# The low rope-key product of two neighbouring heads as 64-row products on the two halves of the array

## The chip, the cores and the metric

The kernel runs on one core of one Trainium2 chip. The time is the device time of one execution in microseconds (us); the time before is the median of three runs. A core has a matrix engine (PE, which loads weights, called PEld in the profile, and then streams columns through them), VectorE (DVE), ScalarE (ACT), GpSimd (POOL) and SyncE (SP), which only issues transfers here. Each engine works through its own list in order, and waits where an instruction needs another engine's result.

## The reference

One layer of a mixer with two groups of heads; 1024 latent tokens, 128 context tokens, 256 cached keys. The part that the change touches is the attention of the latent tokens, four heads of 128 plain and 64 rotary dimensions:

```python
def one_block(i):                       # 128 queries
    for qr, (kn, kr, _) in zip(q_ropes, key_sets):
        ...
        logits.append(jnp.einsum('bqhn,bkhn->bhqk', qn, kn)
                      + jnp.einsum('bqhr,bkr->bhqk', qrb, kr))
    s = jnp.concatenate(logits, axis=-1).astype(jnp.float32) * ATTN_SCALE
    p = jax.nn.softmax(s, axis=-1).astype(v_all.dtype)
    return jnp.einsum('bhqk,bkhv->bqhv', p, v_all)
```

The rotary key `kr` is one for all four heads. The first key set are the 1024 latent keys (rotated), the second the 256 cached ones (not rotated). Around this stand a projection, a gated position mixing and an output projection, which do not change.

## The kernel before

**Numbers in two parts.** Products run on values rounded to a short form (F32R). To keep precision each operand is split into a high and a low part, and a product is made of high x high, high x low and low x high.

**The score operands.** For each block `t` of 128 queries and each head `h`, `qnh` and `qnl` hold the high and low part of the query, already carried into the latent space of the keys (128 rows). `qr` holds both parts of the 64 rotary dimensions on top of one another in 128 rows: an even head has the high part in rows 0 to 63 and the low one in rows 64 to 127, an odd head the other way round. `kch` and `kcl` are the parts of the latent key; `krh` and `krl` hold the parts of the rotary key, each of them twice, in rows 0 to 63 and again in 64 to 127. So the product of `qr` with `krh` gives high x high and low x high at once, and the one with `krl` gives high x low and, beside it, low x low. `logits` makes these five products into one bank of PSUM, the accumulator memory.

**The steps.** `score_steps(t, h)` gives the steps of one head: `lat(0)` and `lat(1)` for the two halves of 512 latent keys, into a tile `s1` of two banks (two such tiles are in turn, so a head's tile is needed again two heads later), and `con` for the 256 cached keys, into its half of the one tile `s2`. `softmax` sets up what follows on the other engines, to be recorded some time later by a planning clock (`later(dt, fn)`): DVE takes the maximum of the latent scores (`start`, L1440), then that of the cached ones and the bias `nb` (`shift`, L1443 to L1448), ACT two exponentials into `e` (L1458: 256 columns, then 1024), DVE the reciprocal of the sum, POOL the division (L1463).

**The values.** `value_steps` handles a pair of heads: five times four transposes of `e` (L1524, tile `pT`), which ACT copies to `ph` (L1528) and DVE subtracts to `pl` (L112), six value products into `o` (L1548 to L1550), and at the end a product with `wuv` (L1567, tile `at`).

**The order.** The order on each engine is the one in which the steps are recorded; no scheduler moves it. There are 32 heads, eight query blocks of four. The scores run ahead: `merged` lays the scores of one pair of heads between the value steps of an earlier pair, in proportion to the planned cost of each step. In the same stage ACT, DVE and POOL also prepare the output projection's weights (tiles `traw`, `thi`, `wor`), which SP loads.

Of the kernel before, what the change touches and what calls it, by code (L numbers as in the profile page):

```python
# [9 lines left out]
F32 = mybir.dt.float32  # L10
# [8 lines left out]
P = 128  # L19
# [6 lines left out]
CTX0 = 9 * P  # L26
# [68 lines left out]
def tile_hymba_step(ctx: ExitStack, tc: tile.TileContext, I, O):  # L95
    nc = tc.nc
    V, S, G, T = nc.vector, nc.scalar, nc.gpsimd, nc.tensor

    def opened(name, bufs=1, space=None, side=None):
        kw = dict(name=name, bufs=bufs, reuse_waits="tile")  # L100
        if space is not None:
            kw["space"] = space
        if side is not None:
            kw["side"] = side
        cm = tc.tile_pool(**kw)
        return cm, cm.__enter__()

    def closed(cm):
        cm.__exit__(None, None, None)
# [57 lines left out]
    def later(dt, fn):  # L167
        waiting.append((now[0] + dt, fn))
        waiting.sort(key=lambda w: w[0])
# [42 lines left out]
    def merged(a, b):  # L212
        ta, tb = sum(x for x, _ in a) or 1.0, sum(x for x, _ in b) or 1.0
        ia = ib = 0
        da = db = 0.0
        while ia < len(a) or ib < len(b):
            if ib >= len(b) or (ia < len(a) and da / ta <= db / tb):
                da += a[ia][0]
                run(a[ia])
                ia += 1  # L220
            else:
                db += b[ib][0]
                run(b[ib])
                ib += 1
# [403 lines left out]
    with tc.manual_schedule(engines=engines):  # L628
        keep_warm(WARM0)
        start = Plan()  # L630
# [598 lines left out]
    qnh, qnl, qr = {}, {}, {}  # L1229
# [12 lines left out]
    rot = {}  # L1242
# [114 lines left out]
    if True:  # L1357
# [25 lines left out]
        kch = kv.tile([P, 11 * P], F32R, tag="kch", name="kch")  # L1383
        kcl = kv.tile([P, 11 * P], F32R, tag="kcl", name="kcl")
        krh = kv.tile([P, 11 * P], F32R, tag="krh", name="krh")
        krl = kv.tile([P, 11 * P], F32R, tag="krl", name="krl")
# [36 lines left out]
    c_ps, pss = opened("pss", bufs=2, space=PSUM)  # L1423
# [4 lines left out]
    s2 = pss.tile([P, 2, 256], F32, tag="s2", name="s2", bufs=1)  # L1428

    def softmax(t, h, lat_, con_):  # L1430

        m = sm.tile([P, 2], F32, tag="m", name=f"m{t}{h}", bufs=3)
        nb = sm.tile([P, 1], F32, tag="nb", name=f"nb{t}{h}", bufs=3)
        su = sm.tile([P, 2], F32, tag="su", name=f"su{t}{h}", bufs=3)
        rs = sm.tile([P, 1], F32, tag="rs", name=f"rs{t}{h}", bufs=3)
        e = ap_.tile([P, 1280], F32, tag="e", name=f"e{t}{h}", bufs=6)
        es[t, h] = e

        def start():
            V.tensor_reduce(m[:, 0:1], lat_, axis=AX.X, op=ALU.max)  # L1440

        def shift():
            V.tensor_reduce(m[:, 1:2], con_, axis=AX.X, op=ALU.max)  # L1443
            if units or t < 2 or (t, h) == (NS - 1, 3):
                V.tensor_reduce(nb, m, axis=AX.X, op=ALU.max)
                V.tensor_scalar(nb, nb, nscl[:, t : t + 1], None, op0=ALU.mult)  # L1446
            else:
                V.scalar_tensor_tensor(nb, m[:, 0:1], m[:, 1:2], nscl[:, t : t + 1], op0=ALU.max, op1=ALU.mult)  # L1448
            apart = t > 0
            last = (t, h) == (NS - 1, 3)  # L1450
            later(0.5 if last else 1.2 if apart else 0.6, lambda: exp(0))
            later(2.3 if apart else 0.6, lambda: exp(1))
            later(3.9 if apart else 3.1 if t == 0 else 2.5, divide)
            later(1.3, lambda: spare_lo(1))

        def exp(i):
            src, sl = ((con_, slice(1024, 1280)), (lat_, slice(0, 1024)))[i]
            S.activation(e[:, sl], src, AF.Exp, bias=nb, scale=scl[:, t : t + 1], accum_out=su[:, i : i + 1])  # L1458

        def divide():  # L1460
            V.tensor_tensor(rs, su[:, 0:1], su[:, 1:2], op=ALU.add)
            V.reciprocal(rs, rs)
            G.tensor_scalar(e, e, rs, 0.0, op0=ALU.mult, op1=ALU.add)  # L1463
            made.add(("e", t, h))
            spare_hi(1 if his and his[0] in heavy else 2)
            spare_lo(2)
            if units and units[0][0] in traw:
                n_ = 1
                paced[0] += 1
                for i in range(n_):  # L1470
                    unit_of[0](*units.pop(0), 2.2 * i)

        return start, shift

    def logits(ps, qs, sl):
        qh_, ql_, qr_ = qs
        T.matmul(ps, qh_, kch[:, sl], start=True, stop=False)  # L1477
        T.matmul(ps, qh_, kcl[:, sl], start=False, stop=False)  # L1478
        T.matmul(ps, ql_, kch[:, sl], start=False, stop=False)  # L1479
        T.matmul(ps, qr_, krh[:, sl], start=False, stop=False)  # L1480
        T.matmul(ps, qr_, krl[:, sl], start=False, stop=True)  # L1481

    def score_steps(t, h):
        g, j = t // 3, t % 3
        sl = slice(j * P, (j + 1) * P)
        a, b = qnh[g][:, h, sl], qnl[g][:, h, sl]
        unrot = qr[g][:, 1, h, sl]
        c_ = s2[:, h % 2, :]
        rot = qr[g][:, 0, h, sl]
        cell = {}  # L1490

        def lat(half):
            if half == 0:
                cell["s"] = pss.tile([P, 2, 512], F32, tag="s1", name=f"s1{t}{h}", bufs=2)
            logits(cell["s"][:, half, :], (a, b, rot), slice(half * 512, half * 512 + 512))
            if half == 1:
                cell["start"], cell["shift"] = softmax(t, h, cell["s"].rearrange("p a c -> p (a c)"), c_)
                later(1.2, cell["start"])

        def con():  # L1500
            logits(c_, (a, b, unrot), slice(CTX0, CTX0 + 256))
            later(0.95 if t else 0.7, cell["shift"])

        return [(1.08, lambda: lat(0)), (1.08, lambda: lat(1)), (0.55, con)]

    otile = {}

# [67 lines left out]
    whole = [area[g].rearrange("p a c -> p (a c)") for g in range(3)]  # L1575
# [19 lines left out]
    def spare_hi(n):  # L1595
        for _ in range(min(n, len(his))):
            his.pop(0)()

    def spare_lo(n):
        for _ in range(min(n, len(los))):  # L1600
            los.pop(0)()
# [46 lines left out]
    LEAD = 2  # L1648
# [70 lines left out]
    heads = [(t, h) for t in range(NS) for h in range(4)]  # L1719
# [19 lines left out]
    def value_stream(pair, drain=False):  # L1739
        it = value_steps(*pair)  # L1740
        steps = []
        for i in range(it[0]):
            steps.append((0.44, lambda i=i: it[1](i)))
            items.append((it, i, i == it[0] - 1))
            advance(steps)
        if drain:
            advance(steps, drain=True)
        return steps

    with tc.manual_schedule(engines=engines):  # L1750
# [79 lines left out]
        def t_load(u):  # L1830
            k, c = divmod(u, 2)
            raw = traw[u] = tp.tile([P, 4, 256], F32, tag="raw", name=f"traw{u}", bufs=2)
            for i, row in enumerate((k, k + 4)):
                nc.sync.dma_start(raw[:, 2 * i : 2 * i + 2, :], I["w_o"][row].rearrange("p (s c) -> p s c", s=2)[:, :, 256 * c : 256 * c + 256])
# [81 lines left out]
                T.matmul(ps, b, woh[k][:, c0:c1], start=False, stop=k == NK - 1)  # L1916

        own = own_steps()
        first = [s_ for i in range(LEAD) for s_ in score_steps(*heads[i])]
        merged(first[:4] + own[:1] + [(0.45, lambda: q_rope_T(7))] + first[4:], [])  # L1920
        for c in range(len(pairs)):
            sc = [s_ for i in (2 * c + LEAD, 2 * c + LEAD + 1) if i < len(heads) for s_ in score_steps(*heads[i])]
            if c == 0:
                sc = sc[:3] + own[1:2] + sc[3:5] + own[2:3] + sc[5:]
            if not sc:
                break
            if c == 1:
                vs = value_stream(pairs[0])
                merged(sc[:2] + own[3:] + vs[:1] + sc[2:3] + vs[1:2] + sc[3:5], [])
                merged(vs[2:], sc[5:])  # L1930
            else:
                merged(sc, value_stream(pairs[c - 1]) if c > 0 else [])
            if 2 * c + LEAD + 1 == 5:
                closed(c_ra)
                c_tp, tp = opened("tp", side="left")
                for u in range(2):
                    t_load(u)
                units += [(u, part) for u in range(8) for part in range(2)]
                unit_of.append(t_unit)
            if 2 * c + LEAD + 1 == 27:  # L1940
                first_jobs()
            if 2 * c + LEAD + 1 == 23:
                for k in range(3):
                    wo_piece(2 + k, *flat[1][2 * k : 2 * k + 2])
# [167 lines left out]
    for q in range(3, len(queue)):  # L2112
        n, name, _ = queue[q]
        cell = {}
        ready = {"S1": "s0", "S2": "s1", "S3": "s2", "S4": "s3"}.get(name)
        deps = [f"{ready}{n}"] if ready and n else []
        room = [name_of(q - 3)]
# [274 lines left out]
```

## Time and profile before

| | |
|---|---|
| median of three runs | 604.39 us (603.84 to 604.91) |
| profiled execution | 604.54 us |
| its span, first to last instruction | 602.8 us |
| granted clock of PE | 0.998 |
| heads 6 to 29 in it | 335.89 to 480.59 us |

The span is what the profile covers; the execution's own time has a little around it. The page lists busy times by engine and groups of instructions by line, operation and tile, written output<-input. The timeline shows single instructions, start and duration in microseconds. The list of waits names who waited for whom, with the total, the count and the longest. Durations of products are modelled to their ends and overlap, so that the distance between two starts tells what one costs in a row. "Issue" is idle time for which no wait shows.

### The profile page before, as it was taken

Reading aid. Unit: us, or ns where it says so; the run is one execution under the profiler, and the core shown is the slowest. Engines: PE = TensorE matmul, PEld = TensorE weight load, DVE = VectorE, ACT = ScalarE, POOL = GpSimd, SP = SyncE. Lnnn points to the kernel's source line nnn. Section 1 sums busy time; section 2 is a strip of 40 time slices with the busy share of each in tenths; the row PEclk is TensorE's granted clock in tenths of the full one; section 3 lists DMA queues with packets and bytes.
Section 4 is the critical chain, followed back from the end, with each engine's and each line's share of the span. In section 5 each row is a group of like instructions: output and inputs, shape, how many; then the busy total and the mean of one; then the engine's idle time right before and its main releaser. Section 6 shows DMA issues by size and latency. Waiting matters only on the chain.

```text
span 602.8 us, 10190 instructions
## 1 busy us (share of the span) xinstructions
PE 592.7 (98%) x3661; PEld 535.6 (89%) x3661; DVE 427.1 (71%) x940; ACT 333.5 (55%) x773; POOL 213.5 (35%) x251
## 2 busy tenths in 40 slices
PE   8999999999999999999999999999999999999995
PEld 8578889999989999999998999999999998888884
DVE  3666888967646368476678677777788876477885
ACT  6565886434323245455567657665656463457543
POOL 2462103200000000343264254545434447259834
PEclk9999999999999999999999999999999999999999
DMA  8992001032052134100002033434232028951444
GB/s 309 375 348 93 1 2 70 1 139 71 18 201 79 55 93 139 41 1 1 1 8 71 1 120 109 149 116 152 76 125 102 1 71 293 368 177 38 143 147 162
DMA packets 31059, 67.33 MB, mean 112 GB/s; under 512 B 3344, under 2 KB 17440, under 8 KB 29984
## 3 DMA queue, kind: packets, MB, share of 16 engines
q1 hardware_dynamic: 27792, 55.93, 26.6%
q0 software_dynamic: 2352, 8.39, 4.1%
q10 hardware_dynamic: 864, 2.36, 1.2%
q8 instruction: 29, 0.48, 0.3%
q14 instruction: 22, 0.18, 0.1%
HBM read 53.45 MB, written 13.21 MB: 111 GB/s over the span
## 4 chain that ended last, share of the span: by engine, by line
PE 91%; DMA 3%; DVE 2%; POOL 2%; ACT 1%; issue 1%; SPq 0%; POOLq 0%; ACTq 0%
PE p L916 14%; PE tp L937 7%; PE pT L1524 5%; PE s L1477 3%; PE s L1478 3%; PE s L1480 3%; PE s L1479 3%; PE s L1481 3%; PE o L1548 3%; PE o L1549 3%; PE o L1550 3%; PE zacc L1349 2%; PE zacc L1348 2%; PE zacc L1350 2%; PE S L1886 2%; PE S L1885 2%
## 5 line engine op out<-in xcount | busy, mean ns | idle before, releaser
L1463 POOL TENSOR_SCALAR e<-e,rs 128x1280 f32<-128x1280 f32 x32 | 47.2, 1474 | 99.0 <-ACT ph L1528 51.7
L112 DVE TENSOR_TENSOR pl<-pT,ph 128x512 fp32r<-128x512 f32 x81 | 55.5, 687 | 31.3 <-ACT ph L1528 31.3
L1528 ACT CAST ph<-pT 128x512 fp32r<-128x512 f32 x80 | 47.2, 590 | 50.6 <-PE pT L1524 50.0
L1458 ACT ACTIVATE e<-s,nb,scl 128x256 f32<-128x256 f32 x64 | 56.9, 890 | 26.0 <-DVE nb L1446 17.3
L1196 POOL TENSOR_TENSOR kr<-z,rope 128x64 f32<-128x64 f32 x8 | 2.6, 326 | 155.3 <-ACT z L1205 155.3
L937 PE MATMUL tp<-area,w 128*128 128x384 f32 x288 | 52.5, 337 | 0.0
L937 PEld LDWEIGHTS tp<-area,w 128*128 128x128 f32 x288 | 50.4, 188 | 0.0
L1548 PE MATMUL o<-ph,vh 128*128 128x256 f32 x160 | 48.4, 302 | 0.0
L1524 PE MATMUL pT<-ident,e 128*128 128x128 f32 x320 | 47.9, 272 | 0.0
L1549 PE MATMUL o<-pl,vh 128*128 128x256 f32 x160 | 45.0, 281 | 0.0
L1550 PE MATMUL o<-ph,vl 128*128 128x256 f32 x160 | 44.9, 281 | 0.0
L1440 DVE TENSOR_REDUCE m<-s 128x1 f32<-128x1024 f32 x32 | 38.9, 1215 | 2.6 <-PE s L1481 2.6
L1524 PEld LDWEIGHTS pT<-ident,e 128*128 128x128 f32 x320 | 37.7, 140 | 2.6
L1477 PE MATMUL s<-kch,area 128*128 128x512 f32 (+2 forms) x100 | 39.2, 392 | 0.0
L1478 PE MATMUL s<-kcl,area 128*128 128x512 f32 (+2 forms) x100 | 35.4, 354 | 0.0
L1480 PE MATMUL s<-krh,area 128*128 128x512 f32 (+2 forms) x100 | 35.3, 353 | 0.0
L1479 PE MATMUL s<-kch,area 128*128 128x512 f32 (+2 forms) x100 | 35.1, 351 | 0.0
L1481 PE MATMUL s<-krl,area 128*128 128x512 f32 (+2 forms) x100 | 35.0, 350 | 0.0
L1548 PEld LDWEIGHTS o<-ph,vh 128*128 128x128 f32 x160 | 30.1, 188 | 1.8 <-ACT os L1558 0.2
L1549 PEld LDWEIGHTS o<-pl,vh 128*128 128x128 f32 x160 | 30.2, 189 | 1.3
L1550 PEld LDWEIGHTS o<-ph,vl 128*128 128x128 f32 x160 | 30.1, 188 | 0.0
L916 PE MATMUL p<-area,w 128*128 128x384 f32 x144 | 27.7, 338 | 0.0
(687 smaller groups left out, 1741.4 us busy)
## 6 DMA issues: line engine op xcount, KB each, us to landing
ada<-in_ada_ss SPq DMA_DIRECT2D x16, 512.0 KB, 6.8
w2r<-in_w_t SPq DMA_DIRECT2D x12, 512.0 KB, 4.9
x<-in_x SPq DMA_DIRECT2D x9, 512.0 KB, 8.3
adag<-in_ada_g SPq DMA_DIRECT2D x4, 1024.0 KB, 4.8
traw<-in_w_o SPq DMA_DIRECT2D x16, 256.0 KB, 3.5
tdram<-thi SPq DMA_DIRECT2D x32, 128.0 KB, 1.8
tdram<-traw SPq DMA_DIRECT2D x32, 128.0 KB, 1.9
wor<-in_w_o SPq DMA_DIRECT2D x8, 512.0 KB, 3.7
```

Of the source, the lines that this page charges most:

```text
L112: V.tensor_tensor(lo, src, f32(hi), op=ALU.subtract)
L916: T.matmul(banks[key], a_, b_, start=k == 0 and m == 0, stop=k == 3 and m == len(passes) - 1)
L937: T.matmul(tps[c, 2][:, :GW], w_[c][:, k, :], x_[k, 2], start=k == 0 and m == 0, stop=k == NK - 1 and m == 2)
L1458: S.activation(e[:, sl], src, AF.Exp, bias=nb, scale=scl[:, t : t + 1], accum_out=su[:, i : i + 1])
L1477: T.matmul(ps, qh_, kch[:, sl], start=True, stop=False)
L1478: T.matmul(ps, qh_, kcl[:, sl], start=False, stop=False)
L1479: T.matmul(ps, ql_, kch[:, sl], start=False, stop=False)
L1480: T.matmul(ps, qr_, krh[:, sl], start=False, stop=False)
L1524: T.transpose(ps[:, w : w + P], es[t, h][:, c * P : (c + 1) * P], ident)
L1548: T.matmul(o, vh[:, kt, :], ph[:, sl], start=c == 0, stop=False)
L1549: T.matmul(o, vh[:, kt, :], pl[:, sl], start=False, stop=False)
L1550: T.matmul(o, vl[:, kt, :], ph[:, sl], start=False, stop=c == n - 1)
```

## The change

For heads 6 to 29 (`FROM`, `UPTO`), twelve of the sixteen pairs, a pair is scored as a whole. `whole` makes four of the five latent products of a head and half; the fifth, with `krl`, becomes `half`: 64 rows of `qr`, those that hold the head's high part (rows 0 to 63 for the even head, 64 to 127 for the odd one), with the same rows of `krl`. The four of them stand in one block, `halves`, between the even head's cached scores and the odd head's latent ones, even and odd in turn. They close the even head's banks and open the odd head's. The low x low part, which the 128-row product had carried along, is left out for the latent keys. The cached keys still go through `logits`. Outside the twelve pairs `plain_steps`, the old code, is used.

```diff
-    def score_steps(t, h):
+    AFTER = 1.7
+    FROM, UPTO = 6, 30
+    def score_steps(t, h0):
+        hs = (h0, h0 + 1)
...
+        def whole(x, ps, c, rot):
+            h = hs[x]
+            a, b, r = qnh[g][:, h, sl], qnl[g][:, h, sl], qr[g][:, 1 - rot, h, sl]
+            T.matmul(ps, a, kch[:, c], start=x == 0, stop=False)
+            T.matmul(ps, a, kcl[:, c], start=False, stop=False)
+            T.matmul(ps, b, kch[:, c], start=False, stop=False)
+            T.matmul(ps, r, krh[:, c], start=False, stop=x == 1)
+        def half(x, ps, c, rot):
+            rows = slice(64 * x, 64 * x + 64)
+            T.matmul(ps, qr[g][rows, 1 - rot, hs[x], sl], krl[rows, c], start=x == 1, stop=x == 0)
+        def halves():
+            e_, o_ = room(0), room(1)
+            for i in range(2):
+                half(0, e_[:, i, :], LATS[i], 1)
+                half(1, o_[:, i, :], LATS[i], 1)
+            after(0)
+            later(0.75, cell["start0"])
+            later(AFTER, cell["shift0"])
...
+        return [
+            *((0.93, lambda i=i: lat(0, i)) for i in range(2)), (0.55, lambda: con(0)), (0.7, halves),
+            *((0.93, lambda i=i: lat(1, i)) for i in range(2)), (0.55, lambda: con(1)),
+        ]
+    def plain_steps(t, h):
...
+    def pair_scores(i):
+        return score_steps(*heads[i]) if FROM <= i < UPTO else [s_ for h in range(2) for s_ in plain_steps(*heads[i + h])]
```

The odd head's maximum and bias are recorded 1.05 and 0.95 behind its last steps (1.2 and 0.95 before). What follows shows the order at the pair of block 2, heads 0 and 1; `s120` and `s121` are their score tiles, `pT10`, `ph10` and `pl10` belong to the pair that is turned into values beside them, `o1` is its output.

PE, the even head's second half, before:

```order
L1477 MATMUL s120_3838<-kch_3222,area0_118 128x512
L1478 MATMUL s120_3838<-kcl_3223,area0_118 128x512
L1479 MATMUL s120_3838<-kch_3222,area0_118 128x512
L1480 MATMUL s120_3838<-krh_3224,area0_118 128x512
L1481 MATMUL s120_3838<-krl_3225,area0_118 128x512
L1548 MATMUL o0_3642<-ph01_4_3823,vh_3226 128x256
```

and in the changed kernel:

```order
L1503 MATMUL s120_3838<-kch_3222,area0_118 128x512
L1504 MATMUL s120_3838<-kcl_3223,area0_118 128x512
L1505 MATMUL s120_3838<-kch_3222,area0_118 128x512
L1506 MATMUL s120_3838<-krh_3224,area0_118 128x512
L1586 MATMUL pT10_1_3871<-ident_75,e10_3572 128x128
```

The product with `krl` is gone from the run of five, and a group of transposes that stood ahead of it now stands behind.

PE, behind the even head's cached scores (`s2`), before:

```order
L1480 MATMUL s2_3381<-krh_3224,area0_118 128x256
L1481 MATMUL s2_3381<-krl_3225,area0_118 128x256
L1548 MATMUL o1_3927<-ph10_0_3852,vh_3226 128x256
L1549 MATMUL o1_3927<-pl10_0_3853,vh_3226 128x256
L1550 MATMUL o1_3927<-ph10_0_3852,vl_3227 128x256
```

and in the changed kernel, four transposes later:

```order
L1586 MATMUL pT10_2_3904<-ident_75,e10_3572 128x128
L1586 MATMUL pT10_2_3904<-ident_75,e11_3625 128x128
L1510 MATMUL s120_3838<-krl_3225,area0_118 128x512
L1510 MATMUL s121_3912<-krl_3225,area0_118 128x512
L1510 MATMUL s120_3838<-krl_3225,area0_118 128x512
L1510 MATMUL s121_3912<-krl_3225,area0_118 128x512
L1610 MATMUL o1_3929<-ph10_0_3851,vh_3226 128x256
```

The four 64-row products stand between the transposes and the value products, and they write the two heads' tiles in turn.

DVE, the even head's maximum (`m20`) and bias (`nb20`), before:

```order
L1440 TENSOR_REDUCE m20_3879<-s120_3838 128x1
L1461 TENSOR_TENSOR rs13_3801<-su13_3800 128x1
L1462 RECIPROCAL rs13_3801<-rs13_3801 128x1
L112 TENSOR_TENSOR traw0_3689<-traw0_3689,thi01_3889 128x512
L112 TENSOR_TENSOR pl10_2_3913<-pT10_2_3907,ph10_2_3912 128x512
L1443 TENSOR_REDUCE m20_3879<-s2_3381 128x1
L1445 TENSOR_REDUCE nb20_3880<-m20_3879 128x1
```

and in the changed kernel:

```order
L1461 TENSOR_TENSOR rs13_3808<-su13_3807 128x1
L1462 RECIPROCAL rs13_3808<-rs13_3808 128x1
L112 TENSOR_TENSOR traw0_3689<-traw0_3689,thi01_3894 128x512
L112 TENSOR_TENSOR pl10_2_3910<-pT10_2_3904,ph10_2_3909 128x512
L1440 TENSOR_REDUCE m20_3917<-s120_3838 128x1
L1443 TENSOR_REDUCE m20_3917<-s2_3381 128x1
L1445 TENSOR_REDUCE nb20_3918<-m20_3917 128x1
```

The maximum of the latent scores went from ahead of the two subtractions to behind them.

More of the change, by code (lines that the diff above doesn't have):

```diff
@@ L1481, in logits, with room, after, lat @@
         T.matmul(ps, qr_, krl[:, sl], start=False, stop=True)
-    def score_steps(t, h):
+    AFTER = 1.7
+    FROM, UPTO = 6, 30
+    LATS = (slice(0, 512), slice(512, 1024))
+    CONS = slice(CTX0, CTX0 + 256)
+    def score_steps(t, h0):
+        g, j = t // 3, t % 3
+        sl = slice(j * P, (j + 1) * P)
+        hs = (h0, h0 + 1)
+        cell = {}
+        def room(x):
+            if x not in cell:
+                cell[x] = pss.tile([P, 2, 512], F32, tag="s1", name=f"s1{t}{hs[x]}", bufs=2)
+            return cell[x]
+        def whole(x, ps, c, rot):
[16 more added lines that the diff above has]
+            later(AFTER, cell["shift0"])
+        def after(x):
+            cell[f"start{x}"], cell[f"shift{x}"] = softmax(t, hs[x], room(x).rearrange("p a c -> p (a c)"), s2[:, x, :])
+        def lat(x, i):
+            whole(x, room(x)[:, i, :], LATS[i], 1)
+            if x and i:
+                after(1)
+                later(1.05, cell["start1"])
+        def con(x):
+            h = hs[x]
+            logits(s2[:, x, :], (qnh[g][:, h, sl], qnl[g][:, h, sl], qr[g][:, 1, h, sl]), CONS)
+            if x:
+                later(0.95 if t else 0.7, cell["shift1"])
+        return [
[3 more added lines that the diff above has]
+    def plain_steps(t, h):
         g, j = t // 3, t % 3
@@ L1918, in tile_hymba_step @@
         own = own_steps()
-        first = [s_ for i in range(LEAD) for s_ in score_steps(*heads[i])]
+        first = pair_scores(0)
         merged(first[:4] + own[:1] + [(0.45, lambda: q_rope_T(7))] + first[4:], [])
         for c in range(len(pairs)):
-            sc = [s_ for i in (2 * c + LEAD, 2 * c + LEAD + 1) if i < len(heads) for s_ in score_steps(*heads[i])]
+            sc = pair_scores(2 * c + LEAD) if 2 * c + LEAD < len(heads) else []
             if c == 0:
```

## The prediction

> **What bounds the kernel now.** I read the page's head first, then PE's waits, then the stretch of the twelve pairs that change, then single instructions in it.
>
> ```profile
> span 602.8 us, 10190 instructions
> PE 592.7 (98%) x3661; PEld 535.6 (89%) x3661; DVE 427.1 (71%) x940; ACT 333.5 (55%) x773; POOL 213.5 (35%) x251
> ```
>
> The matrix engine (PE) is busy for 98% of the span. These are all of its waits in the list of waits:
>
> ```profile
> PE warm L442 <- DVE onesr L239: 1.4, 1, 1.4
> PE modp L337 <- DMA ada<-in_ada_ss: 0.9, 2, 0.5
> PE vacc L436 <- DVE area L112: 0.3, 1, 0.3
> ```
>
> None lies among the scores. The busy times by stretch, from the first product of head 6 to the first of head 30, agree: PE 144.70 of 144.70 us at a granted clock of 1.00, while VectorE (DVE) has 33 us to spare.
>
> ```profile
> core 0: us, PE busy (x) PEld busy (x) DVE busy (x) ACT busy (x) POOL busy (x), PEclk, DMA share, GB/s
> 335.89:480.59 144.70, 144.70 (x1011) 133.40 (x1010) 111.50 (x234) 89.46 (x183) 65.77 (x69) 1.00 0.30 99
> ```
>
> So a pair of heads takes 144.70 / 12 = 12.06 us, and what changes here is worth what it takes from PE or adds to it, as long as no other engine comes late. A busy PE is not the same as an array without gaps, so I price a product by the distance of starts, not by its duration. Five score products of 512 columns in a row, PE's timeline:
>
> ```profile
> 342.25 0.40 PE L1477 MATMUL s<-kch,area 128*128 128x512 f32 x1
> ...
> 343.18 0.39 PE L1481 MATMUL s<-krl,area 128*128 128x512 f32 x1
> 343.41 0.60 PE L1567 MATMUL at<-os,wuv 128*128 128x128 f32 x4
> ```
>
> From 342.25 to 343.41 are five products: 0.232 us each, though each is shown as 0.39 long; the other 0.16 overlaps the next one.
>
> **The change, part by part.** *Removed:* the low product with krl on all 128 rows, once per head and half, so 4 per pair and 48 in all, which is what the groups of that stretch count:
>
> ```profile
> L1481 PE MATMUL s<-krl,area 128*128 128x512 f32 x48 | 18.7, 390 | 0.0
> ```
>
> 4 x 0.232 = 0.93 us of PE time per pair. *Added:* four products of 64 rows and 512 columns in one block. If the two that lie on different halves of the array run side by side, they make two rounds; if not, four. No 64-row product is in this trace, so I take the nearest rows: the gate products gps (L1014) of another stage, whose weights are only 32 columns wide, so that four fit on the array beside one another. PE's timeline in narrow windows, and the weight loads (PEld) at both borders:
>
> ```profile
> 161.61 1.21 PE L916 MATMUL p<-area,w 128*128 128x384 f32 x6
> 162.49 0.33 PE L916 MATMUL p<-area,w 128*128 128x384 f32 x1
> 162.75 0.42 PE L1014 MATMUL gps<-adag,csp 128*32 128x256 f32 x4
> 162.99 0.61 PE L1014 MATMUL gps<-adag,csp 128*32 128x256 f32 x8
> 163.20 0.61 PE L1014 MATMUL gps<-adag,csp 128*32 128x256 f32 x8
> 163.42 0.40 PE L1014 MATMUL gps<-adag,csp 128*32 128x256 f32 x4
> 163.75 0.44 PE L916 MATMUL p<-area,w 128*128 128x384 f32 x1
> 164.03 0.33 PE L916 MATMUL p<-area,w 128*128 128x384 f32 x1
> 162.75 0.16 PEld L1014 LDWEIGHTS gps<-adag,csp 128*32 128x32 f32 x8 [0.25 <-issue]
> 163.75 0.19 PEld L916 LDWEIGHTS p<-area,w 128*128 128x128 f32 x1 [0.41 <-issue]
> ```
>
> Three things are in these rows. First, strips do run together: four products start within the same 0.02 us, and the rounds follow at 162.99, 163.20 and 163.42, 0.215 us apart, where one of them alone lasts 0.40. Second, going into strips and out again costs time. Plain products come every (1.21 - 0.33) / 5 = 0.176 us. From the last plain start before (162.49) to the second after (164.03) are 1.54 us; two plain steps (0.352) and four rounds (0.86) explain 1.21, so the excursion costs 0.33. Third, the weight loads wait at both borders for the array to run empty (the two "issue" gaps) and are then in the open: the first products last 0.42 instead of 0.40 behind a load of 32 columns, and 0.44 instead of 0.33 behind one of 128. The new block loads 128 columns on both sides, so I add 0.11 - 0.02 = 0.09: 0.42 us per block.
>
> A round is 0.215 by the strips and 0.232 by the score products; nothing decides, so I take the middle, 0.224. One block then costs 2 x 0.224 + 0.42 = 0.87 us against the 0.93 removed. The gain is 0.06 us per pair, 0.7 us over twelve. Bounds: at best 0.93 - 0.43 - 0.33 = 0.17 per pair, 2.0 us in all (load price of the narrow strips); at worst the two halves' weights are loaded one after the other, another 0.11 (0.53 in all), with rounds of 0.232, which loses 0.06 per pair, 0.8 us.
>
> The Trainium skill, "TensorEngine Tiling (Array Packing)", Key Properties, states that changing the tiling mode, as against the tile, drains the engine. The strips' 0.33 us agrees for strips of columns; by that rule halves of rows pay too (my forecast), without it the block is the first rival below.
>
> *Another neighbour.* The block stands between transposes and value products. Passing from transposes to products is free in itself:
>
> ```profile
> 350.20 0.60 PE L1524 MATMUL pT<-ident,e 128*128 128x128 f32 x4
> 350.55 0.48 PE L1477 MATMUL s<-kch,area 128*128 128x512 f32 x1
> 350.87 0.40 PE L1478 MATMUL s<-kcl,area 128*128 128x512 f32 x1
> ```
>
> One transpose of 128 columns follows another after (0.60 - 0.27) / 3 = 0.11 us (0.27 is one alone, its group's mean is 272 ns). Four of them and one product of 0.232 make 0.67, which is 350.87 - 350.20.
>
> *Moved:* the maximum of the even head (L1440). Its scores were complete before its context product; now they are complete behind the block, and DVE takes the maximum behind the third pl instead of ahead of two subtractions. On ACT one thi copy goes ahead of the odd head's large exponential and ph number 1 behind it; POOL and SP keep their orders, so the loads and the POOL work start where they did in the program. Queued behind the later maximum are the bias nb, both exponentials, and behind those the next pair's first product, which needs the score bank. One even head before, PE, DVE and ACT:
>
> ```profile
> 375.69 0.39 PE L1481 MATMUL s<-krl,area 128*128 128x512 f32 x1
> 376.31 1.21 DVE L1440 TENSOR_REDUCE m<-s 128x1 f32<-128x1024 f32 x1
> 377.44 0.15 DVE L1461 TENSOR_TENSOR rs<-su 128x1 f32<-128x1 f32 x1
> ...
> 378.31 0.68 DVE L112 TENSOR_TENSOR pl<-pT,ph 128x512 fp32r<-128x512 f32 x1
> 378.91 0.41 DVE L1443 TENSOR_REDUCE m<-s 128x1 f32<-128x256 f32 x1
> 379.55 0.21 DVE L1446 TENSOR_SCALAR nb<-nb,nscl 128x1 f32<-128x1 f32 x1
> 379.80 0.57 ACT L1458 ACTIVATE e<-s,nb,scl 128x256 f32<-128x256 f32 x1 [1.72 <-DVE nb L1446]
> 381.23 1.21 ACT L1458 ACTIVATE e<-s,nb,scl 128x1024 f32<-128x1024 f32 x1
> 384.11 0.40 PE L1477 MATMUL s<-kch,area 128*128 128x512 f32 x1
> ```
>
> The large exponential ends at 382.44 and PE wants the bank at 384.11: 1.67 us of cover. The pl at 378.31 is tied to its transposes and hardly moves, so the maximum (377.44 - 376.31 = 1.13) now goes between it and 378.91, and nb and both exponentials come 1.13 later. The pair is 0.06 shorter. Cover left: 1.67 - 1.13 - 0.06, about 0.5 us. So I cost the move at nothing; it is thin, and below it each 0.1 us short costs 12 x 0.1.
>
> Sum: 0.7 us less. The profiled execution took 604.54 with a span of 602.8, so 1.7 lie around it, and it stands 0.15 above the median 604.39. From the median: **603.7 us**.
>
> **The rivals.**
> - *No price for the mode.* If halves of rows need no emptying, as the transposes above need none, the block costs only its rounds: 0.93 - 0.45 = 0.48 per pair, 5.8 us, 598.6. For it: both kinds use all 128 columns, and the strips do not. Against it: the strips are the only rows in which the array is divided, and they pay on both sides.
> - *The halves run one after the other* (slower). The strips that ran together wrote different partitions; the two halves write the same 128 partitions in two banks, which nothing here shows. Four products at 0.232 take back all of the 0.93, and the borders add 0.42 x 12 = 5.0 us: 609.4. It decides as soon as a round costs over 0.26 us, (0.93 - 0.42) / 2. Without the price of the borders it would be 604.4.
> - *Rounds longer than one product.* With a round of 1.3 products, 0.30, the block costs 0.60 + 0.42, 0.09 over what was removed: 605.5. The strips' 0.215 speaks against it. The Trainium skill, "TensorE: Matmul & The Clock Gate", Measured speedup vs the span model, gives 3.07x for four row tiles, so three quarters of full packing, which is such a round.
> - *The even head's bank comes late.* If nb is not 1.13 but 1.9 later (a subtraction or two, 0.6 each, ahead of it), PE waits 0.3 us in each of the twelve pairs, 3.6 us: 604.39 - 0.7 + 3.6 = 607.3.
>
> **How the numbers follow.** A measurement of this kernel can tell about 0.2%, 1.2 us, from no change. Forecast 0.50, within 602.4 to 605.2; about 0.14 of that lies beyond 1.2 us faster, the rest within. No price 0.20, faster. One after the other 0.13: 0.10 slower, 0.03 without borders, the same. Late bank 0.12: 0.08 slower, 0.04 so little that it is the same. Longer rounds 0.05: 0.03 the same, 0.02 slower. That makes faster 0.34, same 0.46, slower 0.20. The range goes down to the first rival with rounds of 0.215 (6.0 us, 598.4) and up to the rival of longer rounds and a small wait, 605.8; outside are the serial halves (0.10) and the larger waits (about 0.06).
>
> **What would show it.** Right: 48 products of the new line in pairs that start together, pairs 0.22 us apart; a gap marked "issue" on PEld ahead of the block and behind it, and a first product longer by about 0.1 on both sides; pairs of 12.0 us where they were 12.06; no PE wait on ACT's e. Wrong: starts 0.23 us apart one by one (serial); no gap at the borders and pairs near 11.6 us (no price); PE waiting for e L1458 or its new line (late bank).

## The result, and the profile after

The changed kernel takes 602.36 us (median of 6 runs, 602.10 to 602.78) against 604.42 (6 runs, 603.84 to 605.37): the ratio is 0.9964, 95% interval 0.9954 to 0.9974. That is 2.1 us or 0.34% faster; the forecast was 603.7. The profiled execution has a span of 600.4 us, 2.4 less than before.

The head of the page, all of PE's waits, and the busy times from the first product of head 6 to the first of head 30:

```profile
span 600.4 us, 10191 instructions
PE 590.3 (98%) x3661; PEld 528.2 (88%) x3661; DVE 427.3 (71%) x940; ACT 329.2 (55%) x773; POOL 214.0 (36%) x251
...
PE warm L442 <- DVE onesr L239: 1.4, 1, 1.4
PE modp L337 <- DMA ada<-in_ada_ss: 0.6, 1, 0.6
PE vacc L436 <- DVE area L112: 0.4, 1, 0.4
PE w L1977 <- DVE kcl L112: 0.2, 1, 0.2
...
335.58:478.08 142.50, 142.50 (x1010) 125.95 (x1009) 110.64 (x234) 85.60 (x183) 65.36 (x68) 1.00 0.31 101
```

The stretch of the twelve pairs is 142.50 us where it was 144.70, and PE is still busy in all of it. These 2.20 us are the result; the other 0.2 of the span are 0.3 less ahead of the stretch, which starts at 335.58 and not at 335.89, and 0.1 more behind it, in code that is the same. A pair takes 11.87 us, where it took 12.07 in most pairs, 12.22 in one and 11.99 in the last ones.

One block on PE's timeline. The rows of the block are from narrow windows, so that its two rounds can be told apart; the last two rows show the weight loads on PEld, of the block and of the first product behind it:

```profile
375.99 0.60 PE L1586 MATMUL pT<-ident,e 128*128 128x128 f32 x4
376.52 0.50 PE L1510 MATMUL s<-krl,area 64*128 64x512 f32 x2
376.86 0.40 PE L1510 MATMUL s<-krl,area 64*128 64x512 f32 x2
377.18 0.39 PE L1610 MATMUL o<-ph,vh 128*128 128x256 f32 x1
377.41 0.28 PE L1611 MATMUL o<-pl,vh 128*128 128x256 f32 x1
376.52 0.30 PEld L1510 LDWEIGHTS s<-krl,area 64*128 64x128 f32 x4 [0.17 <-issue]
377.18 0.19 PEld L1610 LDWEIGHTS o<-ph,vh 128*128 128x128 f32 x1 [0.36 <-ACT os L1620]
```

The halves start two by two (that the array works on both at once is what e3 tests). The transposes need until 375.99 + 4 x 0.11 = 376.43; from there to the second value product are 0.98 us, of which 0.12 is that value product's own step. So a block costs 0.86 us. Its first border is seen twice: nothing starts between 376.43 and 376.52, and the first round is 0.50 long where the second is 0.40. The 0.10 is the weight load in the open. The first round without its load, 0.34 - 0.10, gives 0.24 for a round at the rounding of these rows; unrounded it is 0.234, and the borders are 0.86 - 0.47 = 0.39. The second border is seen twice as well: the second round needs until 376.86 + 0.23 = 377.09, the value product starts at 377.18, and it is 0.39 long where the next is 0.28. Here the profile names not "issue" but the copy os, in eight of the twelve pairs; whether that is a wait of its own is what e10 tests.

### The profile page after: what moved, and what is told of

It reads as the page before. It is cut to its first block, busy times and chain, and to the rows that moved or that the text cites. A ratio compares the mean times of both kernels' runs of the same rounds, so it can differ in the third digit from the quotient of the medians.

```text
span 600.4 us, 10191 instructions
## 1 busy us (share of the span) xinstructions
PE 590.3 (98%) x3661; PEld 528.2 (88%) x3661; DVE 427.3 (71%) x940; ACT 329.2 (55%) x773; POOL 214.0 (36%) x251
## 4 chain that ended last, share of the span: by engine, by line
PE 93%; DMA 3%; DVE 2%; ACT 1%; POOL 1%; issue 0%; SPq 0%; POOLq 0%; ACTq 0%
PE p L916 14%; PE tp L937 7%; PE pT L1586 6%; PE o L1610 3%; PE o L1612 3%; PE o L1611 3%; PE zacc L1349 2%; PE zacc L1348 2%; PE zacc L1350 2%; PE S L1947 2%; PE S L1948 2%; PE S L1949 2%; DMA ada<-in_ada_ss 2%; PE s L1503 2%; PE s L1506 2%; PE s L1505 2%
## 5 line engine op out<-in xcount | busy, mean ns | idle before, releaser
L1610 PE MATMUL o<-ph,vh 128*128 128x256 f32 x160 | 50.7, 317 | 0.0
L916 PE MATMUL p<-area,s 128*128 128x384 f32 x144 | 27.3, 337 | 0.0
L1348 PE MATMUL zacc<-w1t,area 128*128 128x448 f32 x72 | 27.1, 376 | 0.0
L916 PE MATMUL p<-w1t,s 128*128 128x384 f32 x144 | 26.9, 339 | 0.0
L1349 PE MATMUL zacc<-w1t,area 128*128 128x448 f32 x72 | 26.3, 366 | 0.0
L1350 PE MATMUL zacc<-w1t,area 128*128 128x448 f32 x72 | 26.3, 365 | 0.0
```

The source lines that it names most:

```text
L916: T.matmul(banks[key], a_, b_, start=k == 0 and m == 0, stop=k == 3 and m == len(passes) - 1)
L1348: T.matmul(ps[:, :448], a, wqh[k], start=k == 0, stop=False)
L1610: T.matmul(o, vh[:, kt, :], ph[:, sl], start=c == 0, stop=False)
```

## The experiments

Two theories stood at the start. A: the two-round block saves 0.07 us per pair, and the rest of the 2.2 us comes from the new order. B: all of it is due to the halves. A second look at the trace of before gave A its place. Behind the even head's cached scores, PE, PEld and ACT:

```profile
377.55 0.28 PE L1481 MATMUL s<-krl,area 128*128 128x256 f32 x1
377.66 0.37 PE L1548 MATMUL o<-ph,vh 128*128 128x256 f32 x1
377.87 0.28 PE L1549 MATMUL o<-pl,vh 128*128 128x256 f32 x1
377.64 0.19 PEld L1548 LDWEIGHTS o<-ph,vh 128*128 128x128 f32 x1
376.70 0.62 ACT L1847 CAST thi<-traw 128x512 fp32r<-128x512 f32 x1
377.21 0.38 ACT L1558 COPY os<-o 128x256 f32<-128x256 f32 x1
```

The value product L1548 takes 0.21 us to the next and not 0.12. Its weights load at 377.64, just after the end, at 377.59, of the copy os, which frees the tile `o`; os stood behind a thi copy on ACT. The product looks 0.09 longer, which counts as busy, so no wait shows. That os holds the load is a reading of these times; e2 tests it. Eight of the twelve pairs have this step of 0.20 to 0.22 us; the others have 0.12. In one of the eight, the pair of 12.22 us, the product also starts 0.14 later.

**e1: the same order with whole rows.**

```diff
-            rows = slice(64 * x, 64 * x + 64)
+            rows = slice(0, 128)
```

> The changed kernel's order word for word, but the four products of the block use all 128 rows (low x low is carried along again), so the array is never divided. Theory (the block itself saves 0.07 us per pair, the new order the rest: no late value product, 0.09 us, and score products a little closer): the block costs 4 x 0.232 = 0.93 instead of 0.86 us, pairs of 11.93 us, 0.8 us more than the changed kernel, 603.2, and so 1.2 us below before. Rival A (all of the gain comes from the halves): 604.4, as before. Rival B (all of it from the order, the halves give nothing): 602.4, as changed.

Measured 603.58 us, ratio to before 0.9986 (0.9977 to 0.9995): 0.9 us less than before and 1.2 more than the changed kernel. Neither rival fits, and the theory's 603.2 is 0.4 too low. The order alone gives 0.9 us, and none of its twelve value products behind the block is late; the halves give the other 1.2. Its block:

```profile
376.15 0.60 PE L1586 MATMUL pT<-ident,e 128*128 128x128 f32 x4
376.51 1.17 PE L1510 MATMUL s<-krl,area 128*128 128x512 f32 x4
377.51 0.28 PE L1610 MATMUL o<-ph,vh 128*128 128x256 f32 x1
377.63 0.28 PE L1611 MATMUL o<-pl,vh 128*128 128x256 f32 x1
```

No gap stands at either border (the start at 376.51, ahead of the last transpose's end, is how plain products follow transposes in the prediction's rows at 350.20), and the value product behind the block is not long. By the same count 377.63 - 0.12 - (376.15 + 0.44) = 0.92 us. The halves' 0.86 saves 0.06 to 0.07, 0.8 us over twelve pairs, and 1.2 was measured. The theory had put "score products a little closer" to the order; e6 shows that it goes with the halves.

**e2: the kernel before with os ahead of thi.** The second thi copy is recorded later, which swaps these two on ACT and nothing else on any engine.

```diff
-            for dt, fn, i in ((3.2, high, 0), (4.6, low, 0), (5.0, high, 1), (6.4, low, 1)):
+            for dt, fn, i in ((3.2, high, 0), (4.6, low, 0), (6.2, high, 1), (6.4, low, 1)):
```

> The kernel before with one edit: ACT copies the output os ahead of the second thi copy, not behind it; all other orders are the same and no product changes. Theory (the first value product behind the even head's cached scores loads its weights late because os frees its bank late): the distance from that product to the next falls from 0.20 to 0.12 us in the nine pairs that have a thi copy, pairs of 12.07 become 11.98, 603.6, 0.8 us less than before. Rival (that distance has another cause, and the gain is the halves'): 604.4.

Measured 603.65 us, ratio 0.9985 (0.9977 to 0.9994), 0.8 us less, as A has it (the pairs that change are eight, not nine; seven gain 0.09 and the one of 12.22 us gains 0.23). The same place:

```profile
377.07 0.28 PE L1481 MATMUL s<-krl,area 128*128 128x256 f32 x1
377.19 0.28 PE L1548 MATMUL o<-ph,vh 128*128 128x256 f32 x1
377.31 0.28 PE L1549 MATMUL o<-pl,vh 128*128 128x256 f32 x1
```

So one swapped pair of copies on ACT in those pairs, with no change to PE's list, is worth about as much as the whole new order of e1.

**e3: both heads on the same half.**

```diff
-            rows = slice(64 * x, 64 * x + 64)
+            rows = slice(0, 64)
```

> The changed kernel, but the odd head's two products of the block lie on rows 0 to 63 too, so that all four use the same half of the array (the odd head's high x low is left out, its low x low is computed). Theory (two rounds, because the halves run side by side): four rounds of 0.234 instead of two, 0.47 us more per pair, 5.6 us in all, 608.0. Rival (the four products take what they take by their count and columns, side by side or not): 602.4, as changed.

Measured 608.33 us, ratio 1.0061 (1.0047 to 1.0074): 6.0 us over the changed kernel, 0.50 per pair. One block; the first row holds its first and second product, the second row the second and third:

```profile
378.19 0.73 PE L1510 MATMUL s<-krl,area 64*128 64x512 f32 x2
378.52 0.63 PE L1510 MATMUL s<-krl,area 64*128 64x512 f32 x2
379.31 0.38 PE L1610 MATMUL o<-ph,vh 128*128 128x256 f32 x1
```

The products start one by one: from 378.19 to 379.31 are 1.12 us, where the changed kernel has 377.18 - 376.52 = 0.66, so 0.46 more. Two rounds became four. That two halves run side by side is shown, and that a half by itself takes as long as whole rows. The rest of the 0.50 is for the most part the wider spacing of e6.

**e4: twice as many borders.** The even head's krh product of its second half is moved into the block.

```diff
             for i in range(2):
+                if i:
+                    T.matmul(e_[:, 1, :], qr[g][:, 0, h0, sl], krh[:, LATS[1]], start=False, stop=False)
                 half(0, e_[:, i, :], LATS[i], 1)
```

> The changed kernel, but one 128-row product (the even head's krh product of its second half) is moved from its run of four to between the two rounds of the block, so that PE goes from whole to halves and back twice per pair; the number of products is the same. Theory (a change of mode costs at both borders, 0.39 us an excursion): 0.39 x 12 = 4.7 us more, 607.1. Rival (the price is paid once per block for another reason, its semaphores or the transposes ahead of it): 602.4, as changed.

Measured 607.55 us, ratio 1.0050 (1.0034 to 1.0065): 5.2 us more than the changed kernel, 0.43 per excursion; about 0.3 us of it is the wider spacing of e6, which leaves 0.41. Both the halves and the moved product now wait and load in the open:

```profile
377.66 0.50 PE L1511 MATMUL s<-krl,area 64*128 64x512 f32 x2
378.09 0.51 PE L1517 MATMUL s<-krh,area 128*128 128x512 f32 x1
378.52 0.50 PE L1511 MATMUL s<-krl,area 64*128 64x512 f32 x2
378.95 0.39 PE L1613 MATMUL o<-ph,vh 128*128 128x256 f32 x1
...
PEld s L1511 <- issue: 5.0, 24, 0.2
PEld s L1517 <- issue: 2.9, 12, 0.2
```

Steps of 0.43 instead of 0.23, and an "issue" gap ahead of each of the 24 rounds and of the twelve moved products.

**e5: no block.** The four products of the block are left out, and with them the high x low part for the latent keys.

> The changed kernel without the block: the high x low rotary product of the latent keys is left out in the twelve pairs, all else stands in the same order. Theory (a block costs PE 0.86 us, 0.47 for two rounds and 0.39 for the borders, and hides nothing else): 12 x 0.86 = 10.3 us less than the changed kernel, 592.1, pairs of 11.0 us. Rival (part of the block lies beside other work, or its absence uncovers a wait for the even head's bank, which has some 0.5 us of cover): less is gained, 594 to 598, and PE waits for the exponentials (e) or for os.

Measured 599.44 us, ratio 0.9919 (0.9905 to 0.9932): 2.9 us less than the changed kernel, not 10.3. The theory fell. The rival's mechanism holds, a wait that comes uncovered, and it is the one for os; still less was gained than its 594 to 598. PE's wait in the list, then PE's timeline and ACT's over one pair:

```profile
PE o L1607 <- ACT os L1617: 3.8, 8, 0.6
...
376.34 0.39 PE L1607 MATMUL o<-ph,vh 128*128 128x256 f32 x1 [0.46 <-ACT os L1617]
387.13 0.64 ACT L1906 CAST thi<-traw 128x512 fp32r<-128x512 f32 x1
387.65 0.39 ACT L1617 COPY os<-o 128x256 f32<-128x256 f32 x1
388.09 0.39 PE L1607 MATMUL o<-ph,vh 128*128 128x256 f32 x1 [0.47 <-ACT os L1617]
```

From one such value product to the next are 388.09 - 376.34 = 11.75 us, only 0.12 below the changed kernel's pair. The four pairs without this wait fell to 11.05 to 11.52. The wait for os that the change had covered is back, and as it is longer than what a product overlaps, it shows in PE's list.

**e9: no block, and os ahead of thi** (the edit of e2, with 5.7).

> The kernel without the block once more (high x low rotary product of the latent keys left out in the twelve pairs), and ACT copies os ahead of the second thi copy. Theory (without the block PE waits 0.46 us per pair for os, behind a copy of 0.5 us; this wait, not the block, holds the pairs at 11.76 us): the wait nearly goes, the pairs with a thi copy fall to 11.2 to 11.3 us, 4 us less than without the block alone, 595.4. Rival (ACT's chain as a whole is the bound, or the score banks): another wait takes its place and it stays at 599 us.

Measured 598.71 us, ratio 0.9904 (0.9889 to 0.9919): 0.7 us less than e5, not 4. The waits of the weight loads, and PE at two places of one pair:

```profile
PEld o L1607 <- ACT os L1617: 2.0, 8, 0.4
PEld s L1503 <- ACT e L1458: 1.6, 7, 0.3
...
381.04 0.28 PE L1477 MATMUL s<-kch,area 128*128 128x256 f32 x1
381.82 0.50 PE L1503 MATMUL s<-kch,area 128*128 128x512 f32 x1
...
386.67 0.60 PE L1583 MATMUL pT<-ident,e 128*128 128x128 f32 x4
387.25 0.39 PE L1607 MATMUL o<-ph,vh 128*128 128x256 f32 x1
```

Os still costs 0.14 us of gap (387.25 against 386.67 + 0.44) and 0.11 of a longer product, where it had been 0.46 and as much. But the next pair's first score product now waits for the exponential that frees its bank: five products of 0.12 behind 381.04 end at 381.64, it starts at 381.82 and lasts 0.50 and not 0.40. The pairs with a thi copy take 11.61 us. The expectation named the wait rightly and was wrong on what stands behind it.

**e10: the changed kernel with os ahead of thi** (the same edit).

> The changed kernel with os ahead of the second thi copy. Theory (in the changed kernel the block lies over the wait for os, with some 0.1 us to spare, and PE alone sets the pair's 11.87 us): the same time, 602.3. Rival (part of the empty time behind the block, which the profile puts down to os in eight pairs, is a wait and not the border): up to 0.1 us in eight pairs, 601.5.

Measured 602.16 us, ratio 0.9961 (0.9948 to 0.9973), the same as the changed kernel's. The gap ahead of the first value product, in the changed kernel and here:

```profile
PEld o L1610 <- ACT os L1620: 2.9, 8, 0.4
PEld o L1610 <- ACT thi L1909: 2.9, 8, 0.4
```

In this kernel os is done 0.5 us earlier against the block's start: at the place of the first profile it ends 0.03 us ahead of that start and not 0.48 behind it. The gap is as long and has only another name, so it is the border and not a wait for os. There the block lies over os, and the swap has nothing left to give.

**e8: the block in all 16 pairs** (`FROM, UPTO = 0, 32`).

> The changed kernel with the block in all 16 pairs instead of 12. Theory 1 (a block is worth 0.07 to 0.11 us wherever it stands): 0.3 to 0.4 us less, 602.0. Theory 2 (the first three pairs take 7 to 11 us, not 12, with 0.1 to 1.5 us of cover over the score banks before the change, and a block that completes the even head later takes over 1 us of it): PE waits for the exponentials in the first pairs, some 1 to 3 us, 603 to 605.

Measured 606.79 us, ratio 1.0042 (1.0029 to 1.0054): slower than before by 2.5 and than the changed kernel by 4.4. PE waits 3.0 us for exponentials, in the first pairs:

```profile
PE s L1477 <- ACT e L1458: 2.3, 3, 1.3
PE s L1503 <- ACT e L1458: 0.7, 2, 0.3
```

Theory 2 is right in kind; the loss is larger than its 603 to 605, since head 6 starts at 340.65 and not at 335.58 us. The steps of the 128 context tokens (`own_steps`) are laid by position between the first pairs' steps, which moves them too, so not all of it need be the banks: 3.0 us are PE's waits for the exponentials, and what the other 2 us are is not shown. From head 30 to the end both kernels need 122 us, so the last pair has no part in it.

**e6: the changed kernel once more.**

> The changed kernel once more, for a second profile beside the experiments: its plain score products stood 0.227 us apart in the first profile, against 0.231 to 0.234 in all others with the same order. If that belongs to the kernel it is there again, and 602.4; if it belongs to that one execution, the distance is 0.231 and the stretch of the twelve pairs about 0.3 us longer.

Measured 602.24 us, ratio 0.9965 (0.9952 to 0.9978). The second step in the runs of four plain score products is 0.227 us again on the average, and so it is in e8 and e10 (0.226 and 0.227). In e1, e3, e4, e5 and e9, with the same products, it is 0.231 to 0.232. So it goes with the two-round block that nothing stands in. It makes 10.91 against e1's 11.13 us over the 48 second steps and 10.94 against 11.01 over the 48 third ones, about 0.3 us in all, and with it 0.8 + 0.3 of the 1.2 us between e1 and the changed kernel are told. Why the products stand closer there is open.

## Why the prediction was right

The sign and the place were right, and the block was priced nearly to the hundredth, but the forecast of 0.7 us was a third of what came, because one gain was missing from the sum and a second, smaller one came that is still unexplained. The measured 602.36 lies at the edge of the 602.4 to 605.2 that the prediction gave to its own forecast.

- *The block:* forecast 0.87 us, measured 0.86. Rounds were taken at 0.224 and are 0.234; the borders at 0.42 and are 0.39, so the two errors nearly cancel. The step from strips of columns to halves of rows held, the 128-column loads in the open on both sides too (0.10 and 0.11 seen, 0.11 taken).
- *The round was right in part by luck.* The strips' 0.215 us stood for a round of 512 columns, but their products have 256, for which a plain score product needs 0.12. The strips multiply plain F32 tiles (`csp`, `ada`), and the trace has two rows for each such product. Per column 0.215 / 256 is 0.84 ns, about what the F32 product `at` takes on the whole array (0.11 for 128 columns a row, 0.86 ns) and not the 0.45 ns of the score products (0.232 / 512). So the strips do show that a round takes as long as one product of its kind, but 0.215 next to 0.232 is a coincidence of 256 columns at one pace and 512 at the other.
- *The first rival, no price for the mode,* is excluded by the gaps at the borders and by e4: 0.43 us for each further excursion. The rule of the Trainium skill, "TensorEngine Tiling (Array Packing)", Key Properties, that a change of mode drains the engine, holds here for halves of rows as well. e5 suggests besides that even without a price it would not have given all of its 0.48, a pair of 11.58 us: with no block at all, the eight pairs held by os took 11.76 to 11.90. No run has the rounds without the borders.
- *Serial halves* and *longer rounds* are excluded by the paired starts, the rounds of 0.234 and e3. The speedup of 3.07x for four row tiles in the Trainium skill, "TensorE: Matmul & The Clock Gate", Measured speedup vs the span model, did not carry over to two halves: two took the time of one (0.234 against 0.232). No run here has four row tiles.
- *The late bank:* the cover was put at 0.5 us and is 0.56. The even head's large exponential now ends at 382.59 and PE wants the bank at 383.15:

```profile
381.37 1.22 ACT L1458 ACTIVATE e<-s,nb,scl 128x1024 f32<-128x1024 f32 x1
383.15 0.40 PE L1503 MATMUL s<-kch,area 128*128 128x512 f32 x1
```

- *The step that failed* is "None lies among the scores", read from the list of PE's waits and from 144.70 busy of 144.70. There was one, 0.09 us in seven pairs and 0.23 in one, 0.8 us in all by e2, and the new order covers it by putting the block, or in e1 its whole-row products, ahead of the waiting product. The sentence that a busy PE is not an array without gaps stood next to it; the pair's 12.06 us should have been added up from its steps, 20 x 0.232 + 10 x 0.119 + 20 x 0.109 + 30 x 0.118 + 4 x 0.11 = 11.99, and the difference looked for. With it, and with the new order read to cover it, the forecast would have been 1.5 us, and 602.9.
- The remaining 0.3 us are the closer score products of e6, which no row of before could have shown.

## What to carry to other kernels

Add up an engine's steps from the distances of starts and compare the sum with the time of one round of the loop: what is left over are waits that count as busy, and one of them may be worth more than the products that a change removes. Dividing the array pays only when the rounds saved outweigh two borders (here 0.93 - 0.47 = 0.46 us saved against 0.39), so more half products behind one change of mode should pay better; that was not run. Before taking more from the engine that is the bound, find the next bound: here one stood 0.1 us and another 0.3 us below the pair's 11.87 in eight of the pairs, and taking 0.86 us per pair from PE brought 2.9 us instead of 10.3.

## What the runs showed of the hardware

A product whose weights load late has no wait of its own in the profile: it is shown longer (0.37 for 0.28) and as busy; only a later one (0.46 us in e5) shows as a wait. A change between whole rows and halves costs 0.39 us there and back, of which 0.21 are the two weight loads that nothing covers and the rest two gaps of 0.09 in which nothing starts. Two products on different halves of the rows, writing the same 128 partitions in two banks, start within 0.004 us of one another and take the time of one (0.234); on the same half they take twice that. Not expected, and open, is that plain products of 512 columns elsewhere in the pair stand closer in the kernels with such a block (the second step of four 0.227 instead of 0.231 us).
